# A hybrid attention and recurrence layer on one core: three heads of values in 512 columns, aligned pools, new costs for the placing clock

## The chip, the cores and the metric

The kernel runs on one core of a Trainium2 chip. The metric is device time in microseconds (us) from start to end of one launch. A core has TensorE (PE, matrix products into the banks of PSUM), VectorE (DVE), ScalarE (ACT), GpSimd (POOL) and SyncE (SP); PE's weight loads (PEld) run beside its products, and DMA queues move data between the chip's memory and SBUF.

## The reference

One layer over 512 latent tokens and 256 context tokens of width 2048, in float32:

```python
parts = split(hn @ w_in)                 # hn: modulated rmsnorm of latent or context tokens
q, k, v = heads(parts[0..2])             # 4 heads, 256 wide for q and k, 512 for v
o_gla, s_f, s_b = gla_bidir(q, k, v, la_f, la_b, s0_f, s0_b)
y_rnn = rglru_bidir(depthwise_conv(parts[6]), ...)      # 16 blocks of 128 channels
o = rmsnorm(o_gla) * silu(parts[3])
y = sigmoid(parts[8] + b) * (o @ w_o_gla) + sigmoid(parts[9] + b) * ((y_rnn * silu(parts[7])) @ w_o_rnn)
x = rmsnorm(x + gt_x * (y @ w_out)) * g_final
```

The modulation (`sh`, `sc`, `gt`) is a product of a conditioning vector with a 2048 by 6144 matrix. Context tokens pass the projection, the attention and the recurrence too, and their final states start the latent scans.

## The kernel before

Every large product is made of three: both operands are split into a high and a low part, and `mm3` issues high by high, low by high, high by low. Weights come as pieces of 128 x 1024 (512 KB): `run` loads a piece into `raw` (two buffers), ScalarE copies it rounded (`whi`), VectorE takes the difference (`wlo`), both in a `ring` of three, two pieces ahead of use. In the trace `L90` is any ScalarE activation, `L94` any VectorE tensor-tensor, `L127` any product through `mm`, so the tiles tell operations apart. A row `px<-whi,xhi ... 128x256` is a product into the bank `px` with 256 columns of `whi` streaming past tokens that are the loaded weights; `px<-xhi,whi` has tokens streaming.

The order on TensorE is the program's. It runs: the start (token norms, modulation, keys); a first phase with recurrent inputs (`g_feat`), values (`g_tok`, W_V: four token blocks of latents in two `px` banks, context in one `pc` bank, 256 columns, so eight groups for four heads), pieces of the gate matrix; the GLA phase from `to_gla` on; from `swap` on the two output projections; the final projection (`g_final`, four blocks of 512 columns). `VALUES_AT` says behind which of the eight recurrent groups the value groups come.

Beside it, side steps (`rnn_block`, `gate_row`, `gla_all`, generators) are put between two products where the products `yield`. `run_side` decides by a clock `T` of its own: each operation adds a cost in `_op`, and a step is taken when its inputs are ready by that clock. `need` and `flush_side` force the steps that are left: `to_gla` flushes at the end of the first phase, `swap` ahead of the first piece of `y`.

Side steps that matter here: a recurrent block makes two gates, each by three products `rx` and three `rc` into the single banks `sa` and `sb`, which a sigmoid (`g<-rx`) frees. `evac_v` copies values to staging tiles `vt` (two buffers) and stores them to `vS`. `gate_row` sums a weighted matrix (`pr<-gacc`, bank `sa`), copies it to `grow` (one buffer) and stores it to `rS`. `gla_out` makes a head's output (`po`), its norm (`ors`), scales it (`on`), transposes it (`pt`) and multiplies it into `sgg`.

Of the kernel before, what the change touches and what calls it, by code (L numbers as in the profile page):

```python
# [44 lines left out]

VALUES_AT = [(), (0,), (1,), (2,), (3,), (4,), (), (5, 6, 7)]

# [7 lines left out]
class Kern:  # L55
# [39 lines left out]

    def ts(self, out, in0, s1, s2=None, op0=ALU.mult, op1=None):
        self._op("dve", self._n(out) / 960.0 + 0.08, out, in0, s1)
        if op1 is None:
            return self.nc.vector.tensor_scalar(out=out, in0=in0, scalar1=s1, scalar2=None, op0=op0)
        return self.nc.vector.tensor_scalar(out=out, in0=in0, scalar1=s1, scalar2=s2, op0=op0, op1=op1)  # L100

    def stt(self, out, in0, s, in1, op0, op1):
        self._op("dve", self._n(out) / 960.0 + 0.08, out, in0, in1)
        return self.nc.vector.scalar_tensor_tensor(out=out, in0=in0, scalar=s, in1=in1, op0=op0, op1=op1)  # L104

    def scan(self, out, a, u, init):
        self._op("dve", self._n(out) / 480.0 + 0.08, out, a, u)
# [164 lines left out]
    def g_tok(self, w0, evac):  # L272
# [27 lines left out]
        return ps  # L300


    def build(self):
# [31 lines left out]
        self.cp = const.tile([P, 32], F32, name="cp")  # L335
        self.sm = open_pool("sm", bufs=2)

# [16 lines left out]
        def to_rnn():  # L354
            close_pool("raw0")
            close_pool("start")
            late = open_pool("late", bufs=1, side="right")
            self.mask = late.tile([P, 384], F32, name="mask")
            self.lax = late.tile([P, TA], F32R, name="lax")
            nc.gpsimd.memset(self.mask, 1.0)  # L360
            nc.gpsimd.memset(self.mask.rearrange("p (b t) -> p b t", t=P)[:, :, 0:1], 0.0)
            self.rp = open_pool("rnn", bufs=1)
            self.side.append(self.decay_consts())
            self.gacc = self.rp.tile([P, 1024], F32, tag="gacc", name="gacc")

# [3 lines left out]
        for j in range(8):  # L369
            main += self.g_feat(W_R + 4 * j, self.evac_r(j), True)  # L370
            main += self.g_feat(W_GR + 4 * j, self.evac_gr(j), False)
            for i in VALUES_AT[j]:
                main += self.g_tok(W_V + 4 * i, self.evac_v(i))
        gp = self.gate_pieces()
# [85 lines left out]
    def start(self, sp, raw0, raw, prime):  # L460
# [74 lines left out]
        sb_free = [0.0]  # L535
        pr0 = self.ps.tile([P, 4, 2], F32, tag="sb", name="pr")

# [4 lines left out]
        def squares(i, t):  # L542
            if i < 8:
                q = self.ring.tile([P, 1024], F32R, tag="whi", name="sq").bitcast(F32)
                h = self.ring.tile([P, 1024], F32R, tag="wlo", name="sh").bitcast(F32)[:, 0:512]
# [23 lines left out]
        def sums(i, h, r):  # L569

            for j in range(4):
                nc.tensor.matmul(pr0[:, j, :], lhsT=h[:, j * P:(j + 1) * P], rhs=ones[:, 0:2],
                                 start=i == 0 and j == 0, stop=i == 7, skip_group_check=True)
            t = pe("pr", 0.9, r)
            if i == 7:
                rstd(0, pr0, t)
# [7 lines left out]
        def rstd(s, pr, t):  # L584
            n = width[s] // P
            q = sp.tile([P, 4], F32, tag="rq", name="rq")[:, 0:n]
            self.rstd(q, pr[:, :, 0], D, sp.tile([P, 2, 4], F32, tag="rt", name="rt")[:, :, 0:n])
            t = sb_free[0] = at("dve", 0.4, t + 0.1)
            at("act", 0.2, t)
# [5 lines left out]
            t = at("dve", 0.22 * n, t)  # L595
            hot.append((lambda: max(t, sb_free[0]), lambda: spread(s, g, t)))

        def spread(s, g, r):

            w = width[s]  # L600
            pr = self.ps.tile([P, w], F32, tag="sb", name="pr")
            nc.tensor.matmul(pr, lhsT=ones, rhs=g[:, 0:w], start=True, stop=True)
            t = pe("pr", w / 600 + 0.05, r, sb_free[0])
            nc.scalar.activation(out=rms[s], in_=pr, func=AF.Copy)
            sb_free[0] = tok_ok[s] = at("act", w / 1200 + 0.18, t + 0.1)

# [305 lines left out]
    def evac_v(self, j):  # L912
        def f(c, x0, x1):
            h, o = j // 2, (j % 2) * 256
            for i, t in enumerate((c, x0, x1)):
                s = self.rp.tile([P, 2, 256], F32, tag="stg", name="vt", bufs=2)
# [570 lines left out]
    def g_final(self, j):  # L1487
# [30 lines left out]
        def evac(t, then=None):  # L1518
# [5 lines left out]
            if then:  # L1524
                then()
            self.act(self.junk, xr, AF.Square, accum_out=self.fss[:, t, j:j + 1])
            if j < 3:
                self.tt(xr, xr, self.gf[:, c0:c0 + 512], ALU.mult)

        held = []  # L1530
        for pi in range(8):
            def mm(hi, lo, pi=pi):
# [8 lines left out]
                if j == 0:  # L1541
                    loads(pi)
                if j == 0 and pi == 6:
                    nc.gpsimd.tensor_tensor(out=self.gt, in0=self.gt, in1=self.gb, op=ALU.add)
                if j == 3 and pi >= 5:
                    held.append((pi, hi, lo))
                    if pi == 7:
                        rest = None
                        for t in range(4):
# [5 lines left out]
                for t in range(4):  # L1555
                    mm_k(t, pi, hi, lo)

            def post():
                if j < 3:
                    for t in range(4):  # L1560
                        evac(t)
                if j == 2:

                    f = self.fss
                    self.fsum = self.sm.tile([P, 4], F32, tag="fsum", name="fsum")
                    self.tt(self.fsum, f[:, :, 0], f[:, :, 1], ALU.add)
                    self.stt(self.fsum, self.fsum, EPS * D, f[:, :, 2], ALU.add, ALU.add)
            ps.append(Piece(a["w"][W_OUT + 8 * j + pi], mm, post if pi == 7 else None))
# [33 lines left out]
def pack(i):  # L1602
# [14 lines left out]
    c = lambda a, b: w_in[:, a:b]  # L1617
    w = np.concatenate([
        c(1024, 2048).reshape(KT, P, 1024), g256(c(2048, 4096)), g256(c(6176, 8224)), g256(c(8224, 10272)),
        g256(c(0, 1024)), g256(c(4096, 6144)), g256(c(10272, 12320)), g256(c(12320, 14368)),  # L1620
# [54 lines left out]
```

## Time and profile before

| | |
|---|---|
| median of three runs | 2302.43 us (2301.64 to 2302.9) |
| profiled execution | 2307.69 us |
| its span, first to last instruction | 2306.0 us |
| mean granted TensorE clock | 0.997 |
| busy: PE, PEld, DVE, ACT, POOL | 99%, 84%, 50%, 44%, 5% |
| mean DMA rate over the span | 131 GB/s |

The span is what the views below show; the profiled execution is 5.26 us longer than the median. TensorE is nearly always busy, so its own waits, and the distances between the starts of its products, are what to read.

### The profile page before, as it was taken

What the parts mean: (1) busy time and instruction counts of PE and PEld (TensorE: products, weight loads), DVE (VectorE), ACT (ScalarE), POOL (GpSimd) and SP (SyncE); (2) the same over time, 40 slices, a digit from 0 to 9 for tenths busy, and PEclk for the clock granted to TensorE, in tenths of its full rate; (3) what the DMA queues carried; (4) which work ended last, traced back from release to release, by engine and by line L of the source; (5) the groups of instructions that cost most, each with busy time, mean ns of one, the idle gap of its engine ahead of it and who ended that gap; (6) DMA issues with size and microseconds to landing.
All of it is one profiled execution on the core that took longest, in us unless ns stands there. A gap on an engine that the chain in (4) does not pass through costs nothing. (4 is left out here: it accounts for less than half of the span.)

```text
span 2306.0 us, 29334 instructions
## 1 busy us (share of the span) xinstructions
PE 2275.4 (99%) x12064; PEld 1928.6 (84%) x12064; DVE 1163.2 (50%) x1494; ACT 1016.3 (44%) x1334; POOL 105.5 (5%) x201
## 2 busy tenths in 40 slices
PE   8999999999999999999999999999999999999998
PEld 5588889989898988998888888888888888888786
DVE  3563245655566555646637637647623432443335
ACT  4343255454454455456556555555533312222223
POOL 0010000000000000000000000000000000000000
PEclk9999999999999999999999999999999999999999
DMA  9943222333333332233233233323335533334423
GB/s 392 375 165 127 92 79 90 129 120 110 105 106 128 124 112 81 100 113 115 90 106 124 83 106 127 119 74 110 132 114 197 192 123 115 127 113 150 173 101 119
DMA packets 85814, 303.02 MB, mean 131 GB/s; under 512 B 10416, under 2 KB 11568, under 8 KB 84784
## 3 DMA queue, kind: packets, MB, share of 16 engines
q1 hardware_dynamic: 72656, 255.78, 32.0%
q0 software_dynamic: 13024, 45.37, 5.5%
q8 instruction: 94, 1.54, 0.3%
q14 instruction: 40, 0.33, 0.0%
HBM read 270.69 MB, written 30.42 MB: 131 GB/s over the span
## 5 line engine op out<-in xcount | busy, mean ns | idle before, releaser
L94 DVE TENSOR_TENSOR wlo<-raw,whi 128x1024 fp32r<-128x1024 f32 x304 | 371.9, 1224 | 568.1 <-ACT whi L90 566.8
L90 ACT ACTIVATE whi<-raw 128x1024 fp32r<-128x1024 f32 x304 | 321.0, 1057 | 529.8 <-PE px L127 327.3
L127 PE MATMUL px<-xhi,whi 128*128 128x512 f32 x1408 | 551.5, 392 | 0.0
L127 PE MATMUL px<-xhi,wlo 128*128 128x512 f32 x1408 | 549.1, 390 | 0.0
L127 PE MATMUL px<-xlo,whi 128*128 128x512 f32 x1408 | 548.1, 389 | 0.0
L127 PEld LDWEIGHTS px<-xhi,wlo 128*128 128x128 f32 x1408 | 264.2, 188 | 57.5 <-DVE wlo L94 0.2
L127 PEld LDWEIGHTS px<-xhi,whi 128*128 128x128 f32 x1408 | 264.4, 188 | 53.9 <-issue 2.6
L127 PEld LDWEIGHTS px<-xlo,whi 128*128 128x128 f32 x1408 | 264.5, 188 | 51.6
L127 PE MATMUL px<-whi,xhi 128*128 128x256 f32 x512 | 144.8, 283 | 0.0
L127 PE MATMUL px<-wlo,xhi 128*128 128x256 f32 x512 | 144.8, 283 | 0.0
L127 PE MATMUL px<-whi,xlo 128*128 128x256 f32 x512 | 144.7, 283 | 0.0
L90 ACT ACT_TABLE_LOAD x100 | 128.3, 1283 | 1.7
L127 PE MATMUL px<-whi,mhi 128*128 128x512 f32 x256 | 100.7, 393 | 2.3 <-ACT whi L90 2.3
L127 PE MATMUL px<-wlo,mhi 128*128 128x512 f32 x256 | 101.0, 394 | 0.8 <-DVE wlo L94 0.8
L127 PE MATMUL px<-whi,mlo 128*128 128x512 f32 x256 | 100.7, 393 | 0.0
L127 PE MATMUL px<-yhi,whi 128*128 128x512 f32 x256 | 99.6, 389 | 0.0
L127 PE MATMUL px<-ylo,whi 128*128 128x512 f32 x256 | 99.6, 389 | 0.0
L127 PE MATMUL px<-yhi,wlo 128*128 128x512 f32 x256 | 99.6, 389 | 0.0
L127 PE MATMUL px<-ohi,whi 128*128 128x512 f32 x256 | 99.6, 389 | 0.0
L127 PE MATMUL px<-olo,whi 128*128 128x512 f32 x256 | 99.6, 389 | 0.0
L127 PE MATMUL px<-ohi,wlo 128*128 128x512 f32 x256 | 99.6, 389 | 0.0
L127 PEld LDWEIGHTS px<-wlo,xhi 128*128 128x128 f32 x512 | 98.1, 192 | 0.2
(327 smaller groups left out, 3963.6 us busy)
## 6 DMA issues: line engine op xcount, KB each, us to landing
raw<-in_w SPq DMA_DIRECT2D x304, 512.0 KB, 3.6
araw<-in_wss SPq DMA_DIRECT2D x35, 512.0 KB, 8.9
raw<-in_wgt SPq DMA_DIRECT2D x32, 512.0 KB, 4.2
tok<-in_wss SPq DMA_DIRECT2D x29, 512.0 KB, 8.9
kraw<-in_w POOLq DMA_DIRECT2D x16, 512.0 KB, 3.9
gS<-mst POOLq DMA_DIRECT2D x32, 256.0 KB, 2.5
gst<-gS POOLq DMA_DIRECT2D x32, 256.0 KB, 3.0
vS<-vt POOLq DMA_DIRECT2D x24, 256.0 KB, 2.6
```

The costliest lines, as they stand in the source:

```text
L90: return self.nc.scalar.activation(out=out, in_=in_, func=func, **kw)
L94: return self.nc.vector.tensor_tensor(out=out, in0=in0, in1=in1, op=op)
L127: self.nc.tensor.matmul(out, lhsT=lhsT, rhs=rhs, start=start, stop=stop, skip_group_check=True)
```

## The change

It has five parts. Values: heads 0, 1 and 3 are made by a new `g_head`, whose four latent and two context token blocks each fill a bank with 512 columns and which yields between products; head 2 stays two narrow groups. The groups come behind other recurrent groups than before. The clock's costs: VectorE and ScalarE operations and products are counted longer. Pools: `sm` goes to the other side of SBUF, the recurrent pool's tiles are allocated ahead in an order of sizes and a filler tile is dropped, so that the context tokens and the recurrent and GLA tiles start at other addresses. Start: the squares of two token tiles are added before they are summed on TensorE. Final projection: gains and biases of the residual are loaded and added earlier, and squares and gain products of the first three blocks become a side step.

```diff
-VALUES_AT = [(), (0,), (1,), (2,), (3,), (4,), (), (5, 6, 7)]
+VALUES_AT = [(), (("w", 0),), (), (("w", 1),), (), (("n", 4),), (), (("w", 3), ("n", 5))]
...
-        self._op("act", self._n(in_) / 1200.0 + 0.2 + sw, out, in_)
+        ap = sum(not isinstance(kw.get(k, 0.0), (int, float)) for k in ("scale", "bias"))
+        self._op("act", self._n(in_) / 1200.0 + 0.2 + 0.07 * ap + sw, out, in_)
...
-        self._op("dve", self._n(out) / 960.0 + 0.08, out, in0, in1)
+        self._op("dve", self._n(out) / 960.0 + 0.16, out, in0, in1)
...
-        self._op("pe", (n / 2400.0 + 0.003 if n >= 256 else 0.213) / share, out, lhsT, rhs)
+        self._op("pe", (n / 2400.0 + 0.0135 if n >= 256 else 0.213) / share, out, lhsT, rhs)
...
+    def g_head(self, w0, evac):
...
+                if pi == 0:
+                    st["o"] = [self.px.tile([P, 512], F32, tag="px", name="px") for _ in range(4)] + \
+                              [self.pc.tile([P, 512], F32, tag="pc", name="pc") for _ in range(2)]
+                for t in (0, 1, 4, 2, 3, 5):
+                    xh, xl = (self.xhi, self.xlo) if t < 4 else (self.chi, self.clo)
+                    t0 = (t % 4) * P
+                    for kk in range(2):
+                        if t or kk:
+                            yield
+                        k = 2 * pi + kk
+                        self.mm3(st["o"][t], (xh[:, k, t0:t0 + P], xl[:, k, t0:t0 + P]),
+                                 (hi[:, kk * 512:(kk + 1) * 512], lo[:, kk * 512:(kk + 1) * 512]), k == 0, k == KT - 1)
+                    if pi == 7:
+                        evac(t, st["o"][t])
...
-        self.sm = open_pool("sm", bufs=2)
+        self.sm = open_pool("sm", bufs=2, side="right")
...
-            yp.tile([P, 240], F32, name="fill")
...
-                nc.vector.tensor_tensor(out=h, in0=q[:, 0:512], in1=q[:, 512:1024], op=ALU.add)
-                f = at("dve", 0.7, e)
-                hot.append((lambda: f, lambda: sums(i, h, f)))
+                if i % 2 == 0:
+                    half.append(self.ring.tile([P, 1024], F32R, tag="wlo", name="sh").bitcast(F32)[:, 0:512])
+                    nc.vector.tensor_tensor(out=half[0], in0=q[:, 0:512], in1=q[:, 512:1024], op=ALU.add)
+                    at("dve", 0.7, e)
+                else:
+                    h = half.pop()
+                    for u in (q[:, 0:512], q[:, 512:1024]):
+                        nc.vector.tensor_tensor(out=h, in0=h, in1=u, op=ALU.add)
+                        f = at("dve", 0.7, e)
+                    hot.append((lambda: f, lambda: sums(i, h, f)))
...
+    def evac_head(self, h):
+        def f(t, x):
+            s = self.rp.tile([P, 512], F32, tag="stg", name="vt", bufs=2)
+            self.act(s, x)
+
+            self.nc.gpsimd.dma_start(out=self.vS[h, :, (t + 2) % 6, :], in_=s)
+        return f
...
-            row = self.rp.tile([1, 512], F32, tag="grow", name="grow")
+            row = self.rp.tile([P, 512], F32, tag="grow", name="grow")[0:1]
...
+            if pi == 0:
+                nc.sync.dma_start(out=self.gt, in_=self.rS.partition_broadcast(P))
+            elif pi == 1:
+                nc.sync.dma_start(out=self.gb, in_=a["bgt"].partition_broadcast(P))
             elif pi == 4:
-                nc.sync.dma_start(out=self.gt, in_=self.rS.partition_broadcast(P))
-            elif pi == 5:
-                nc.sync.dma_start(out=self.gb, in_=a["bgt"].partition_broadcast(P))
-            elif pi == 6:
                 nc.sync.dma_start(out=self.gf, in_=a["gfin"].partition_broadcast(P))
...
-            self.act(self.junk, xr, AF.Square, accum_out=self.fss[:, t, j:j + 1])
-            if j < 3:
+            if j == 3:
+                self.act(self.junk, xr, AF.Square, accum_out=self.fss[:, t, j:j + 1])
+
+        def squares():
+
+            c0 = j * 512
+            for t in range(4):
+                xr = self.xres[:, t, c0:c0 + 512]
+                self.act(self.junk, xr, AF.Square, accum_out=self.fss[:, t, j:j + 1])
                 self.tt(xr, xr, self.gf[:, c0:c0 + 512], ALU.mult)
+                yield 0
...
-                if j == 0 and pi == 6:
+                if j == 0 and pi == 3:
                     nc.gpsimd.tensor_tensor(out=self.gt, in0=self.gt, in1=self.gb, op=ALU.add)
...
                 for t in range(4):
                     mm_k(t, pi, hi, lo)
+                    yield
...
+                    self.side.append(squares())
```

The end of the first phase on TensorE, before: the last recurrent group lies among 256-column products of the last value group.

```order
L127 MATMUL px<-whi,xhi 128x256
L127 MATMUL px<-wlo,xhi 128x256
L127 MATMUL px<-whi,xlo 128x256
L127 MATMUL rx<-xh,wh 128x512
L127 MATMUL rx<-xl,wh 128x512
L127 MATMUL rx<-xh,wl 128x512
L127 MATMUL rc<-xh,wh 128x256
L127 MATMUL rc<-xl,wh 128x256
L127 MATMUL rc<-xh,wl 128x256
L127 MATMUL px<-whi,xhi 128x256
L127 MATMUL px<-wlo,xhi 128x256
L127 MATMUL px<-whi,xlo 128x256
```

Now, on the same engine, the last context product is followed by two groups one behind the other, and then (below these rows) by the first GLA piece:

```order
L129 MATMUL pc<-whi,clo 128x256
L129 MATMUL rx<-xh,wh 128x512
L129 MATMUL rx<-xl,wh 128x512
L129 MATMUL rx<-xh,wl 128x512
L129 MATMUL rc<-xh,wh 128x256
L129 MATMUL rc<-xl,wh 128x256
L129 MATMUL rc<-xh,wl 128x256
L129 MATMUL rx<-xh,wh 128x512
L129 MATMUL rx<-xl,wh 128x512
L129 MATMUL rx<-xh,wl 128x512
L129 MATMUL rc<-xh,wh 128x256
L129 MATMUL rc<-xl,wh 128x256
```

ScalarE at this place now: the copies of values and a split stand ahead of the sigmoids of the two groups (`g_7997` of the first, `g_8008` of the second).

```order
L92 ACTIVATE vt<-pc 128x512
L92 ACTIVATE vt<-px 128x512 x2
L92 ACTIVATE whi<-raw 128x1024
L92 ACTIVATE g_7997<-rx,par 128x512
L92 ACTIVATE g_7997<-rc,par 128x256
L92 ACTIVATE g_8008<-rx,par 128x512
L92 ACTIVATE g_8008<-rc,par 128x256
L92 ACTIVATE sgr<-gr 128x512
```

The end of GLA on TensorE, before: behind the last `po` come 30 products, the last of them here, then eight transposes of the fourth head, and the other eight in two places further on.

```order
L127 MATMUL px<-xhi,whi 128x512
L127 MATMUL px<-xlo,whi 128x512
L127 MATMUL px<-xhi,wlo 128x512
L1432 MATMUL pt<-ident,on 128x128 x8
L127 MATMUL px<-xhi,whi 128x512
L127 MATMUL px<-xlo,whi 128x512
L127 MATMUL px<-xhi,wlo 128x512
```

Now all sixteen transposes follow the last `po` directly:

```order
L129 MATMUL po<-ht,Ah 128x512 x2
L129 MATMUL po<-ht,Al 128x512
L1490 MATMUL pt<-ident,on 128x128 x16
L129 MATMUL px<-xhi,whi 128x512
L129 MATMUL px<-xlo,whi 128x512
L129 MATMUL px<-xhi,wlo 128x512
```

The two sums of a gate row stand side by side and a recurrent group directly behind them, in both halves; before, products lay between them in the first half.

## Rows read from the trace of the kernel before

**Rows 1.** The list of cores, and the page's part 1 (busy us, share, instructions).
```profile
core 0: 2306.0 us, clock 0.997
PE 2275.4 (99%) x12064; PEld 1928.6 (84%) x12064; DVE 1163.2 (50%) x1494; ACT 1016.3 (44%) x1334; POOL 105.5 (5%) x201
```
**Rows 2.** TensorE's waits: who, for whom, us in total, times, longest.
```profile
PE pr L572 <- DVE sh L548: 7.1, 1, 7.1
...
PE pr L1061 <- ACT grow L90: 0.7, 1, 0.7
```
**Rows 3.** Timeline of TensorE, narrow value products, then final projection: start, us, operation.
```profile
963.24 0.28 PE L127 MATMUL px<-whi,xhi 128*128 128x256 f32 x1
...
969.00 0.28 PE L127 MATMUL pc<-whi,chi 128*128 128x256 f32 x1
...
971.83 0.28 PE L127 MATMUL px<-whi,xhi 128*128 128x256 f32 x1
...
2145.01 0.39 PE L127 MATMUL px<-whi,mhi 128*128 128x512 f32 x1
...
2168.80 0.39 PE L127 MATMUL px<-whi,mhi 128*128 128x512 f32 x1
```
**Rows 4.** Timeline of TensorE, second block of the final projection; in brackets the idle time.
```profile
2169.94 0.39 PE L127 MATMUL px<-whi,mlo 128*128 128x512 f32 x1
2172.60 0.50 PE L127 MATMUL px<-whi,mhi 128*128 128x512 f32 x1 [2.27 <-ACT whi L90]
2173.86 0.80 PE L127 MATMUL px<-wlo,mhi 128*128 128x512 f32 x1 [0.76 <-DVE wlo L94]
...
2179.93 0.40 PE L127 MATMUL px<-whi,mhi 128*128 128x512 f32 x1
```
**Rows 5.** Timeline of VectorE at the first evacuation of the final projection.
```profile
2160.85 0.69 DVE L94 TENSOR_TENSOR yt<-px,gv 128x512 f32<-128x512 f32 x1 [4.49 <-POOL gv L1544]
```
**Rows 6.** One line's instructions; busy time in a stretch, the last three: clock, DMA share, GB/s.
```profile
L572 PE MATMUL pr<-ones,sh x64: 343/353/374, 7.1 to 21.7; 128*128 128x2 f32 x64
...
10.00:20.00 10.00, 10.00 (x52) 9.39 (x52) 3.97 (x6) 5.29 (x5) 0.00 (x0) 1.00 1.03 419
```
**Rows 7.** Timeline of TensorE and ScalarE at 1010 us; waits ahead of tile vt.
```profile
1010.32 0.40 PE L127 MATMUL px<-xhi,whi 128*128 128x512 f32 x1
...
1014.07 0.60 ACT L90 ACTIVATE vt<-px 128x512 f32<-128x512 f32 x1 [2.46 <-DMA vS<-vt]
1014.56 2.27 ACT L90 ACTIVATE whi<-raw 128x1024 fp32r<-128x1024 f32 x2
...
  DMA vS<-vt: 21.5, 8
```
**Rows 8.** Timelines of TensorE and VectorE, output of the fourth head.
```profile
1656.87 0.40 PE L127 MATMUL px<-xhi,whi 128*128 128x512 f32 x1
...
1669.99 1.22 DVE L94 TENSOR_TENSOR ht<-st,ht 128x1024 fp32r<-128x1024 f32 x1
...
1690.94 0.39 PE L127 MATMUL px<-xhi,whi 128*128 128x512 f32 x1
...
1694.44 1.41 DVE L99 TENSOR_SCALAR on<-po,ors 128x512 f32<-128x512 f32 x2
...
1697.76 1.03 PE L1432 MATMUL pt<-ident,on 128*128 128x128 f32 x8
...
1698.39 0.69 DVE L94 TENSOR_TENSOR sgg<-pt,sgg 128x512 f32<-128x512 f32 x1 [1.07 <-PE pt L1432]
```
**Rows 9.** Timelines of TensorE and ScalarE at the gate rows of both halves.
```profile
620.97 0.59 ACT L90 ACTIVATE grow<-pr 1x512 f32<-1x512 f32 x1 [4.33 <-DMA rS<-grow]
...
621.61 0.50 PE L127 MATMUL rx<-xh,wh 128*128 128x512 f32 x1 [1.46 <-ACT grow L90]
...
622.65 0.28 PE L127 MATMUL rc<-xh,wl 128*128 128x256 f32 x1
...
887.57 0.59 ACT L90 ACTIVATE grow<-pr 1x512 f32<-1x512 f32 x1 [1.94 <-DMA rS<-grow]
```

More of the change, by code (lines that the diff above doesn't have):

```diff
@@ L102, in stt @@
     def stt(self, out, in0, s, in1, op0, op1):
-        self._op("dve", self._n(out) / 960.0 + 0.08, out, in0, in1)
+        self._op("dve", self._n(out) / 960.0 + 0.21, out, in0, in1)
         return self.nc.vector.scalar_tensor_tensor(out=out, in0=in0, scalar=s, in1=in1, op0=op0, op1=op1)
     def scan(self, out, a, u, init):
-        self._op("dve", self._n(out) / 480.0 + 0.08, out, a, u)
+        self._op("dve", self._n(out) / 480.0 + 0.16, out, a, u)
         return self.nc.vector.tensor_tensor_scan(
@@ L300, in g_tok, with mk, mm @@
         return ps
+    def g_head(self, w0, evac):
+        st = {}
+        ps = []
+        def mk(pi):
+            def mm(hi, lo):
+                if pi == 0:
[12 more added lines that the diff above has]
+                        evac(t, st["o"][t])
+            return mm
+        for pi in range(8):
+            ps.append(Piece(self.a["w"][w0 + pi], mk(pi)))
+        return ps
     def build(self):
@@ L362, in to_rnn @@
             self.rp = open_pool("rnn", bufs=1)
+            rp = self.rp
+            self.gacc = rp.tile([P, 1024], F32, tag="gacc", name="gacc")
+            for n, w, d, m in (("wh", 512, F32R, 1), ("wl", 512, F32R, 1), ("wr", 512, F32, 1), ("gr", TX, F32, 3),
+                               ("sgr", TX, F32, 2), ("stg", 512, F32, 2), ("grow", 512, F32, 1), ("xr", TA, F32, 3),
+                               ("xh", TA, F32R, 1), ("xc", TA, F32, 1), ("xl", TA, F32R, 1)):
+                rp.tile([P, w], d, tag=n, name=n + "0", bufs=m)
             self.side.append(self.decay_consts())
-            self.gacc = self.rp.tile([P, 1024], F32, tag="gacc", name="gacc")
         pcs[0].before = to_rnn
@@ L371, in build @@
             main += self.g_feat(W_GR + 4 * j, self.evac_gr(j), False)
-            for i in VALUES_AT[j]:
-                main += self.g_tok(W_V + 4 * i, self.evac_v(i))
+            for kind, i in VALUES_AT[j]:
+                if kind == "w":
+                    main += self.g_head(W_V + 8 * i, self.evac_head(i))
+                else:
+                    main += self.g_tok(W_V + 4 * i, self.evac_v(i))
         gp = self.gate_pieces()
@@ L535, in start @@
         sb_free = [0.0]
-        pr0 = self.ps.tile([P, 4, 2], F32, tag="sb", name="pr")
+        pr0 = self.px.tile([P, 4, 2], F32, tag="px", name="pr")
+        half = []
         def load_tok(i, d):
@@ L572, in sums @@
                 nc.tensor.matmul(pr0[:, j, :], lhsT=h[:, j * P:(j + 1) * P], rhs=ones[:, 0:2],
-                                 start=i == 0 and j == 0, stop=i == 7, skip_group_check=True)
-            t = pe("pr", 0.9, r)
+                                 start=i == 1 and j == 0, stop=i == 7, skip_group_check=True)
+            t = pe("pr", 1.87, r)
             if i == 7:
@@ L595, in rstd @@
             t = at("dve", 0.22 * n, t)
-            hot.append((lambda: max(t, sb_free[0]), lambda: spread(s, g, t)))
+            hot.append((lambda: max(t, sb_free[0] if s else 0.0), lambda: spread(s, g, t)))
         def spread(s, g, r):
             w = width[s]
-            pr = self.ps.tile([P, w], F32, tag="sb", name="pr")
+            pool, tag = (self.ps, "sb") if s else (self.px, "px")
+            pr = pool.tile([P, w], F32, tag=tag, name="pr")
             nc.tensor.matmul(pr, lhsT=ones, rhs=g[:, 0:w], start=True, stop=True)
-            t = pe("pr", w / 600 + 0.05, r, sb_free[0])
+            t = pe("pr", w / 600 + 0.05, r)
             nc.scalar.activation(out=rms[s], in_=pr, func=AF.Copy)
-            sb_free[0] = tok_ok[s] = at("act", w / 1200 + 0.18, t + 0.1)
+            tok_ok[s] = at("act", w / 1200 + 0.18, t + 0.4)
+            if s:
+                sb_free[0] = tok_ok[s]
         blocks = START_BLOCKS
@@ L1525, in evac @@
                 then()
-            self.act(self.junk, xr, AF.Square, accum_out=self.fss[:, t, j:j + 1])
-            if j < 3:
-                self.tt(xr, xr, self.gf[:, c0:c0 + 512], ALU.mult)
+            if j == 3:
[5 more added lines that the diff above has]
+                self.act(self.junk, xr, AF.Square, accum_out=self.fss[:, t, j:j + 1])
+                self.tt(xr, xr, self.gf[:, c0:c0 + 512], ALU.mult)
+                yield 0
+            if j == 2:
+                f = self.fss
+                self.fsum = self.sm.tile([P, 4], F32, tag="fsum", name="fsum")
+                self.tt(self.fsum, f[:, :, 0], f[:, :, 1], ALU.add)
+                self.stt(self.fsum, self.fsum, EPS * D, f[:, :, 2], ALU.add, ALU.add)
+                yield 0
         held = []
@@ L1617, in pack @@
     c = lambda a, b: w_in[:, a:b]
+    wv = [(g256 if h == 2 else g512)(c(2048 + 512 * h, 2560 + 512 * h)) for h in range(4)]
     w = np.concatenate([
-        c(1024, 2048).reshape(KT, P, 1024), g256(c(2048, 4096)), g256(c(6176, 8224)), g256(c(8224, 10272)),
+        c(1024, 2048).reshape(KT, P, 1024), *wv, g256(c(6176, 8224)), g256(c(8224, 10272)),
         g256(c(0, 1024)), g256(c(4096, 6144)), g256(c(10272, 12320)), g256(c(12320, 14368)),
```

16 lines of the change are left out of this document (7 added, 9 removed).

## The prediction, on record before the result

> **What bounds the kernel now.** The page's first part and the list of cores say that TensorE is busy 99% of the span at a granted clock of 0.997 [rows 1]. From some 85 us to the end the products follow one another, so a change is worth what it takes off that one stream: fewer or cheaper products, or idle time of that engine. VectorE and ScalarE, at about half the span, matter only where a product waits for them. The list of TensorE's waits, read second, is short: the first product of all waits 7.1 us, no other wait is over 2.5, and of the first phase only the gate sums and what follows them appear [rows 2]. Read third, the timeline of TensorE gives start-to-start distances; the "us" of one matmul overlaps the next and can't be used as a price.
>
> **Values.** Removed: six groups of 256 columns (three heads), 1152 products on the latent tokens and 576 on the context. Forty-eight latent ones take 963.24 to 969.00, 119.9 ns each; twenty-four context ones 969.00 to 971.83, 117.9 ns [rows 3]: 138.1 + 67.9 = 206.0 us. Added: 864 products of 512 columns. None with the weights as moving operand exists in this phase; the nearest are the output projection's (105 from 2145.01 to 2168.80, 226.6 ns [rows 3]): 195.8. Sum **-10** by these rows, -9.7 taken, since places between products cost a few weight switches. Bounds, with the distance two per cent to either side of that row: -14 and -6.
>
> Both widths carry about 13 ns over 256 and 512 columns at 2.4 GHz [rows 3], and it is that overhead which halving the count saves. The Trainium skill, "TensorE: Matmul & The Clock Gate", section "Wait — 56ns, not 53.3ns?", gives a fixed cost of about 2.5 ns for each matmul. By it 864 fewer would be worth 2.2 us instead of 9.7; no row here is that tight.
>
> **Final stage.** Before, the row of the residual's gain came in late; its POOL addition held VectorE 4.49 us, and VectorE began the four evacuations only at 2160.85 [rows 5]; ScalarE's next split stood behind them. TensorE's last product of that block started at 2169.94, the next at 2172.60, the one behind it at 2173.86, and until 2179.93 the clock was at its lower level [rows 4]. Between 2169.94 and 2179.93 sixteen products start; at 226.6 ns that is 3.63 us out of 9.99, so 6.36 are lost: 2.27 and 0.76 are the noted waits, the rest, about 3.2, is the clock. The change loads the gain at the first pieces, adds earlier, and leaves eight VectorE operations of 0.69 (5.5 us) ahead of the split, with squares and multiplication spread between later products. **-6.4** (0 if the early loads delay a split instead; the stream has two pieces of slack).
>
> **Start.** The sums are 64 passes in 7.1 to 21.7 [rows 6], 0.22 us each; 32 fewer would be 6.9. But the transfers run at 1.03 of the 16 engines in the same stretch [rows 6], and the pieces that follow land one by one, so the time freed mostly becomes a wait for them. **-1.5** (0 to -6.9).
>
> **The end of the first phase.** Now the two added parts. The new costs and order move the side steps, and a flush ahead of the GLA piece forces what is left. In the new order two recurrent-block groups (rx, rc) stand back to back behind the last context products, where 256-column products used to lie between groups. The second group needs the bank that the sigmoid of the first frees, and that sigmoid stands on ScalarE behind three copies of values and a split. How long these take is shown in the same place of before: TensorE is free at 1010.32, the third copy starts at 1014.07 (it waits 2.46 for the store of the first, whose staging buffer it takes), and the split at 1014.56 [rows 7]. This wait stands in all eight value groups, 21.5 us together [rows 7], hidden by products. With X for TensorE's first free moment: split at X+4.2, of one piece half the row's 2.27, and the sigmoid, as long as a copy of its shape (0.60) or a little longer, from 5.2 to 5.85; second group at X+5.9, where TensorE was ready at X+1.05: **+4.85** idle. A pause of 2.3 was followed by the lower clock [rows 4], so I add the price from there, **+3.2**. Behind the wait on ScalarE are the exponentials and the next split, needed some 24 us after X by my count and ready then: nothing is added.
>
> **The end of GLA.** Of the same kind. Before, 30 products lay between the last output product (po) of the last head and the first transposes (pt), and more between the transposes. Now the flush ahead of the first y piece puts all 16 transposes directly behind po. The chain to them, from E = 1690.94, the product after po: square, table, root, five small VectorE steps, and the scaling at 1694.44 (two take 1.41) [rows 8], so the first transpose at E+4.3. Then each tile passes transposes, VectorE's product 0.63 us after they start (1697.76, 1698.39) [rows 8], and the next scaling on the same engine, about 1.4 a tile: products resume at E+8.0. Less 1.75 of TensorE's own work: **+6.25**. One clock fall, **+3.2**. Ahead of it, 48 instead of 78 products stand between the last state products and po. The operand that po reads last was made by VectorE from 1669.99 on in 1.22, so ready 14.3 after TensorE left the state products at 1656.87 [rows 8]; 48 products are 10.9, the dozen of po that don't read it 2.7: late by **+0.7** (0 to 3).
>
> **Gate rows.** In before the two sums of a half were six products apart at the first half, adjacent at the second. The second row's copy waited for the store of the first, 4.33 us there and 1.94 at the second half [rows 9]; TensorE lost 1.46 in front of the recurrent group and 0.74 at the second half [rows 2, 9]. Now in both halves both sums and a recurrent group are adjacent. The second sum waits 0.74; the group waits for the gap of store (1.94 to 4.33, of which I take 2.5, the long one being one row), plus 0.59 of copy, less 1.0 of the sum itself: 1.5 to 3.9, taken 2.1. Two halves 5.7, less 2.2: **+3.5** (+2.3 to +7).
>
> **Addresses.** The pools move the context operand and the block weights to the alignment of the latent tokens. Context products at 117.9 ns were 2 ns shorter than the latent ones [rows 3]. If alignment sets that, some 1344 context products get 2.3 ns longer, 3.1; if alignment helps, 1 comes back. **+1.9** (-1 to 3.5). ScalarE's and VectorE's costs in the planner's clock are numbers of the plan alone; their effect is the order above.
>
> **Sum.** -9.7 -6.4 -1.5 +4.85 +3.2 +6.25 +3.2 +0.7 +3.5 +1.9 = +6.0. The profiled execution lasted 2307.69 (span 2306.0), 5.3 above the median of the three runs, and would become 2313.7; on the median, 2302.43 + 6.0 = 2308.4, 0.26% more. Changes below 0.2%, 4.6 us, can't be told from none: faster is below 2297.8, slower above 2307.0.
>
> **Rivals.**
> *The waits come without the clock falling.* The pause of 1.46 at the gate rows was followed by five products in 1.04 us, three wide and two narrow [rows 9], 0.12 more than at the full clock; one of 2.27 was followed by distances of 427 ns [rows 4]. Without the two falls: 2308.4 - 6.4 = 2302.0, no change. For it: the second new wait is broken by transposes. Against: both pauses are longer than the one that had the fall. Chance 0.2.
> *The forced steps find their results ready,* the other side. If the sigmoid is not held by the copies, or the norm of the last head is done under po, the idle and the clock of both places go (-18.2 with the 0.7): 2290.2, faster. It decides from the point where both places together cost less than 7.6 instead of 18.2. For it: before shows no forced step that waits. Against: the copies' wait occurs in all eight groups, and the norm needs the last po. Chance 0.15.
> *The gate rows and the phase's end cost more:* the store at 4.33 in both halves (+3.5), and a fall there or a late second split behind the exponentials (3 to 6): 2315 to 2318. Chance 0.12.
> *The wide products cost almost as much per column as the narrow,* as the page has it: +7.5, 2315.9. Beside the rows at 226.6 ns, chance 0.03.
>
> **How the numbers follow.** Chances: forecast 0.5, the rivals 0.2, 0.15, 0.12, 0.03. The forecast's own range, with start, addresses and the low half at their bounds, is 2302 to 2315; three tenths of it lie below 2307.0, hence 0.15 same and 0.35 slower from it. Same 0.15 + 0.18 = 0.33; slower 0.35 + 0.15 = 0.50; faster 0.17, from the second rival and the start at its full 6.9 beside the first. The range leaves out most of the second rival and the top of the third: 2293 to 2318.
>
> **What would show it.** Values right: distances of 226 to 228 ns in the wide groups, and TensorE's count down by 864 and 32. Final stage: no entry px <- whi or wlo in the list of waits, no lower clock near the second block of the output projection. The end of the first phase: an entry rx <- ACT of some 5 us there, with distances of 427 ns behind it. The end of GLA: pt <- DVE entries that add up to 6 us. Gate rows: rx <- grow twice, about 2 each. Addresses: context products at 120 instead of 118 ns. Start: the first recurrent products no more than 2 us earlier. The prediction is wrong if either flush shows no wait, or if the clock in the rows behind them stays at 2.4 GHz.

## The result: 0.8% slower, three times what was forecast

The changed kernel takes 2322.14 us (median of 4 runs, 2319.36 to 2322.49), the kernel before 2302.66 (4 runs); the ratio is 1.0081, 95% interval 1.0069 to 1.0094, so +15.9 to +21.6 us. The forecast was 2308.4, range 2293 to 2318. The direction and every place that it named were right; the sum was too small and the range ended below the result.

The changed kernel's cores and the page's busy time, in answer to [rows 1]:

```profile
core 0: 2317.7 us, clock 0.995
PE 2268.6 (98%) x11168; PEld 1886.0 (81%) x11168; DVE 1166.1 (50%) x1498; ACT 1019.4 (44%) x1336; POOL 101.1 (4%) x201
```

There are 896 products fewer, TensorE is busy 7 us less, and the span is 11.7 longer: the engine waits more. (The two profiled executions lie 5.0 above and 2.8 below the medians of four runs, hence 11.7 here and 19.5 between the medians.) Its list of waits (who, for whom, us in total, times, longest), in answer to [rows 2]:

```profile
PE pt L1490 <- DVE on L101: 6.7, 3, 4.1
PE rx L129 <- ACT grow L92: 5.5, 2, 3.6
PE rx L129 <- ACT g L92: 4.6, 1, 4.6
...
PE pr L1119 <- ACT grow L92: 1.3, 2, 0.7
PE px L129 <- ACT whi L92: 0.9, 1, 0.9
PE po L129 <- DVE ht L96: 0.8, 1, 0.8
PE pr L1119 <- DVE gacc L106: 0.7, 1, 0.7
```

The three forecast waits stand there by name: `pt <- on` and `rx <- g`, which the kernel before did not have, and `rx <- grow`, which it had at 1.5 us. `po <- ht` is 0.8 where 0.7 was computed. The end of the first phase, ScalarE and then TensorE, answers to [rows 7]:

```profile
1009.41 0.60 ACT L92 ACTIVATE vt<-px 128x512 f32<-128x512 f32 x1 [2.35 <-DMA vS<-vt]
1009.90 1.05 ACT L92 ACTIVATE whi<-raw 128x1024 fp32r<-128x1024 f32 x1
1010.85 0.68 ACT L92 ACTIVATE g<-rx,par 128x512 f32<-128x512 f32 x1
...
1006.70 0.28 PE L129 MATMUL rc<-xh,wl 128*128 128x256 f32 x1
1011.58 0.79 PE L129 MATMUL rx<-xh,wh 128*128 128x512 f32 x1 [4.60 <-ACT g L92]
1012.17 0.63 PE L129 MATMUL rx<-xl,wh 128*128 128x512 f32 x1
...
1014.78 0.39 PE L129 MATMUL px<-xhi,whi 128*128 128x512 f32 x1
```

The copy waits for its staging buffer, the split and the sigmoid follow, and the second recurrent group starts 4.88 after the last product of the first, at the lower clock (0.59 and 0.43 between starts) for 3 us. The end of GLA answers to [rows 8]:

```profile
1714.34 0.39 PE L129 MATMUL po<-ht,Al 128*128 128x512 f32 x1
1718.87 1.97 PE L1490 MATMUL pt<-ident,on 128*128 128x128 f32 x8 [4.15 <-DVE on L101]
1721.43 2.37 PE L1490 MATMUL pt<-ident,on 128*128 128x128 f32 x8 [0.59 <-DVE on L101]
1723.46 0.78 PE L129 MATMUL px<-xhi,whi 128*128 128x512 f32 x1
...
1727.87 0.44 PE L129 MATMUL px<-xlo,whi 128*128 128x512 f32 x1
```

Products resume 8.9 us after the slot behind `po` (1714.57), where E+8.0 was computed, and at the lower clock until 1727.87. The gate rows answer to [rows 9]:

```profile
614.91 0.39 PE L129 MATMUL px<-xhi,wlo 128*128 128x512 f32 x1
616.05 1.02 PE L1119 MATMUL pr<-gacc,ones 128*1 128x512 f32 x2 [0.75 <-DVE gacc L106]
617.75 1.02 PE L1119 MATMUL pr<-gacc,ones 128*1 128x512 f32 x2 [0.68 <-ACT grow L92]
622.37 0.80 PE L129 MATMUL rx<-xh,wh 128*128 128x512 f32 x1 [3.60 <-ACT grow L92]
```

From 614.91 to 622.37 the engine does one product and two sums of 1.02; the rest is the waits of the first sum, the second and the group. The values and the final stage run as planned in the changed kernel (what this is worth against before comes below); the first two rows bound 144 wide products, the last two the whole output projection, in answer to [rows 3, 4]:

```profile
539.98 0.40 PE L129 MATMUL px<-whi,xhi 128*128 128x512 f32 x1
...
572.64 0.39 PE L129 MATMUL rx<-xh,wh 128*128 128x512 f32 x1
...
2133.69 0.39 PE L129 MATMUL px<-whi,mhi 128*128 128x512 f32 x1
...
2307.55 0.39 PE L129 MATMUL px<-whi,mlo 128*128 128x512 f32 x1
```

144 products in 32.66 us are 226.8 ns each; the last stage is 173.86 long without a wait.

To compare executions, the stream is cut at four starts: the first product of the first phase, the first of GLA's queries, the first with `y`, the first of the output projection. Lengths in us, worked out from the timelines:

| | first phase | GLA | y to output | output |
|---|---|---|---|---|
| before, first trace | 800.97 | 757.29 | 348.16 | 180.23 |
| before, second trace (e10) | 799.23 | 757.28 | 348.16 | 174.51 |
| changed, first trace | 804.95 | 771.87 | 348.16 | 173.85 |
| changed, second trace (e9) | 808.49 | 770.15 | 348.16 | 173.85 |
| e2 heads alone | 799.89 | 767.68 | 348.16 | 177.89 |
| e3 costs alone | 802.97 | 772.03 | 348.16 | 175.89 |
| e6 two row buffers | 800.40 | 770.44 | 348.16 | 173.85 |
| e11 changed, old costs | 798.80 | 767.14 | 348.16 | 173.85 |

### The profile page after: what moved, and what is told of

The parts are those of the page before. It is cut to its first block, busy times and chain, and to the rows that moved or that the text cites. A ratio compares the mean times of both kernels' runs of the same rounds, so it can differ in the third digit from the quotient of the medians.

```text
span 2317.7 us, 27573 instructions
## 1 busy us (share of the span) xinstructions
PE 2268.6 (98%) x11168; PEld 1886.0 (81%) x11168; DVE 1166.1 (50%) x1498; ACT 1019.4 (44%) x1336; POOL 101.1 (4%) x201
## 3 DMA queue, kind: packets, MB, share of 16 engines
q8 instruction: 87, 1.43, 0.3%
## 4 chain that ended last, share of the span: by engine, by line
PE 68%; issue 25%; DVE 2%; ACT 2%; DMA 1%; POOL 1%; SPq 0%; DVEq 0%; POOLq 0%; ACTq 0%
PE px L129 53%; PE kx L882 4%; PE po L129 3%; PE kc L882 2%; PE pc L129 2%; PE pa L723 1%; PE pd L129 1%; PE pcs L129 1%; DMA araw<-in_wss 0%; DMA tok<-in_wss 0%; PE rx L129 0%; POOL vS L976 0%; POOL yS L1094 0%; DVE Z L110 0%; DVE wlo L96 0%
## 5 line engine op out<-in xcount | busy, mean ns | idle before, releaser
L129 PE MATMUL px<-whi,xhi 128*128 128x512 f32 (+1 forms) x320 | 111.2, 347 | 0.0
L129 PE MATMUL px<-wlo,xhi 128*128 128x512 f32 (+1 forms) x320 | 111.1, 347 | 0.0
L129 PE MATMUL px<-whi,xlo 128*128 128x512 f32 (+1 forms) x320 | 111.0, 347 | 0.0
L92 ACT ACTIVATE g<-rx,par 128x512 f32<-128x512 f32 x64 | 44.1, 689 | 111.4 <-PE rx L129 111.2
```

## The experiments

The theory is that of the prediction: steps forced behind one another make TensorE wait, and the clock falls behind the wait. Ratios are to the kernel before, run on the same chip.

**e1 to e4: one part of the diff at a time, on the kernel before.** e1 takes the edits of `g_final`, e2 those of `g_head`, `VALUES_AT` and `evac_head`, e3 those of the costs, e4 those of the pools:

```diff
+            if pi == 0:                                              # e1
+                nc.sync.dma_start(out=self.gt, in_=self.rS.partition_broadcast(P))
...
+                    main += self.g_head(W_V + 8 * i, self.evac_head(i))   # e2
...
+        self._op("dve", self._n(out) / 960.0 + 0.16, out, in0, in1)  # e3
...
+        self.sm = open_pool("sm", bufs=2, side="right")              # e4
```

> The kernel before with the part on the final projection alone. Theory (the wait at the second block and the lower clock behind it are lost time in every execution): 6.4 us shorter than before, 2296. Rival (the profiled execution of before, 5 us above its median, shows a fall of the clock that other executions do not have): 2 to 3.5 us shorter, 2299 to 2300.5. No change in the first phase or in GLA by either.

> The kernel before with the wide heads alone, at the old costs of the placing clock and with the old pools. Theory: -10 from the products; a wait of 4 to 5 us at the end of the first phase and one of 6 to 7 us at the end of GLA, both followed by the lower clock (3.2 each); the second pair of gate sums now has a recurrent group behind it, +2. Together +8 to +10: 2311. Rival (the planner's new costs make the waits, the heads only gain): 2293.

> The kernel before with the new costs of the placing clock alone. Theory: the order has all sixteen transposes behind the last output product and both sums of the first gate half side by side: +6.3 +3.2 +0.7 at the end of GLA, +2 to +4 at the gate, no wait at the end of the first phase; +12 to +14, 2315. Rival (costs closer to the measured durations place the steps better): no wait at either place, 2300 to 2303.

> The kernel before with the pools alone (addresses; the order of instructions is that of before). Theory: context products at 120 ns instead of 117.5 to 118, 1536 of them with values and 384 more of keys: +3 to +5, 2306. Rival (addresses cost nothing): 2302.5, within 0.1%. Second rival (they slow VectorE or ScalarE too): over +6.

e1: 2300.79, ratio 0.9990 (0.9981 to 0.9999): -2.3 us, the rival's value. e2: 2313.00, 1.0045 (1.0032 to 1.0057): +10.4, the theory's or a little over it. e3: 2318.34, 1.0065 (1.0051 to 1.0079): +15, a little over it. e4: 2303.82, 1.0006 (0.9997 to 1.0015): +1.4, below the theory's range, within the rival's 0.1% and within the noise. The part on the start has no run of its own. In the list of waits of e2 stand:

```profile
PE pt L1471 <- DVE on L100: 5.0, 2, 4.4
PE rx L128 <- ACT g L91: 4.7, 1, 4.7
...
PE rx L128 <- ACT grow L91: 1.5, 1, 1.5
```

and in that of e3, without any `rx <- g`:

```profile
PE pt L1433 <- DVE on L100: 6.7, 3, 4.1
...
PE rx L128 <- ACT grow L91: 2.1, 1, 2.1
```

The sixteen transposes are forced by either part; the wait at the end of the first phase needs the heads; the third wait of `pt` comes with the costs.

**e9, e10: the changed kernel and the one before, unaltered, for a second trace.**

> The changed kernel once more, for a second trace. Theory: the waits have the same length as in the first trace (rx <- g 4.6, pt <- on 6.7, rx <- grow 5.5), and what differs is how long the lower clock lasts behind them; the span is 2318 to 2321. Rival: another wait is longer by some us, at the start or at a transfer.

> The kernel before once more, for a second trace. Theory: the wait at the second block of the final projection is shorter than the 2.27 and 0.76 of the first trace, without the lower clock behind it, so that the stage from its first product is 175 to 177 us long instead of 180.2. Rival: the stage is as long as in the first trace, and the 5 us between that execution and the median lie at the start.

e9 took 2321.87 (one run); behind the start its waits of over 0.4 us are the first trace's to 0.1 us. The clock differs. A stretch with the second gate half, first trace (after start and end the busy time of five engines, then clock, DMA share, GB/s):

```profile
875.00:888.00 13.00, 10.44 (x44) 6.92 (x44) 2.61 (x3) 4.78 (x9) 1.02 (x2) 1.00 0.34 86
```

and e9:

```profile
880.00:892.00 12.00, 9.52 (x33) 6.05 (x33) 1.23 (x1) 3.90 (x7) 1.01 (x2) 0.86 0.36 104
```

A wait of 1.9 us was followed by the full clock, one of 1.8 by the lower; the first phase is 3.5 us longer in the second trace. e10 took 2301.42 (one run), and its output stage is 174.51, half a us under the expected 175 to 177: one short wait at full clock stands where [rows 4] show the long one.

```profile
2169.61 0.39 PE L127 MATMUL px<-whi,mhi 128*128 128x512 f32 x1
2170.36 0.50 PE L127 MATMUL px<-wlo,mhi 128*128 128x512 f32 x1 [0.36 <-DVE wlo L94]
```

Its gain rows were added on POOL from 2151.74 in 4.60, against 5.55 from 2155.27 in the first trace. POOL and a split on VectorE in the first trace, then in e10:

```profile
2155.27 5.55 POOL L1544 TENSOR_TENSOR gv<-gv 128x2048 f32<-128x2048 f32 x1 [59.49 <-DMA gv<-in_bgt]
2155.14 1.23 DVE L94 TENSOR_TENSOR wlo<-raw,whi 128x1024 fp32r<-128x1024 f32 x1 [4.21 <-ACT whi L90]
...
2151.74 4.60 POOL L1544 TENSOR_TENSOR gv<-gv 128x2048 f32<-128x2048 f32 x1 [56.52 <-DMA gv<-in_bgt]
2154.58 2.85 DVE L94 TENSOR_TENSOR wlo<-raw,whi 128x1024 fp32r<-128x1024 f32 x1 [4.22 <-ACT whi L90]
```

In e10 the DMA ahead of the addition landed earlier, the addition ends 4.5 us earlier, and ScalarE's split behind the evacuations starts 3.5 us earlier (2168.00 against 2171.50).

**e5, e16: the flushes two pieces later, both, and that of `y` alone.**

```diff
-        main[0].before = to_gla
+        main[2].before = to_gla                    # e5
...
-        n = len(main) - 8
-        for i in range(8):
+        n = len(main) - 6                          # e5, e16
+        for i in range(6):
             main.insert(n + 2 * i + 1, cy[i])
...
-                main += g
+                main += [g[0], cy[6], g[1], cy[7], g[2], g[3]]
```

> The changed kernel with both flushes two pieces (48 products, 10.9 us) later: the GLA pools are opened ahead of the third piece of the phase, and the first piece of y is loaded two pieces later. In its order no two recurrent groups stand side by side any more, the third head's first transposes and the second's have more products ahead of them, and 12 products stand between the last output product and the transposes. Theory (the two forced waits, with the clock behind them, and the places of the steps they displace are what the change loses): the entry rx <- g vanishes (-4.9 and 1.3 to 3.2 of clock), pt <- on falls from 6.7 to about 2 to 4, po <- ht vanishes: 12 to 16 us shorter than the changed kernel, 2306 to 2310. Rival (the loss is spread over the stream through addresses and ScalarE's load): 2318 or more.

> The changed kernel with the first piece of y two pieces later and nothing else; its order has 12 products between the last output product and the sixteen transposes, and 84 instead of 48 ahead of that output. Theory: po <- ht vanishes (-1), pt <- on at the last head falls by the 2.7 us that the twelve products take, to 3 to 4, and the lower clock there goes or is shorter: 4 to 7 us shorter than the changed kernel, 2315 to 2318. Rival (the first product of y is late instead): 2320 or more.

e5: 2312.97, 1.0050 (1.0037 to 1.0063), 7 us shorter than the changed kernel by the ratios and 9 by the medians, short of the 12 expected. `rx <- g` is gone, but opening GLA late makes its first product wait (`pz`, 1.3), and the transposes still alternate with VectorE behind their twelve products (5.7 in four waits). e16: 2320.46, 1.0082 (1.0068 to 1.0095), no difference that these runs can tell (3 us to either side), against an expected 4 to 7. In its trace GLA takes 767.6, which is 2.6 to 4.3 less than in the two traces of the changed kernel. More did not come: the first wait at the last head fell from 4.15 to 1.43, but those between the transposes grew from 0.59 to 2.18 (1.74 and 0.44). Twelve products ahead of the chain help little where the chain itself alternates between two engines.

**e6: two buffers for the gate's row.**

```diff
-            row = self.rp.tile([P, 512], F32, tag="grow", name="grow")[0:1]
+            row = self.rp.tile([P, 512], F32, tag="grow", name="grow", bufs=2)[0:1]
```

> The changed kernel with two buffers instead of one for the gate's row; the order of instructions is unchanged. Theory: the recurrent group behind the sums waits for the copies alone, not for the store: rx <- grow falls from 5.5 to about 1.5, and the lower clock behind it goes: 4 to 7 us shorter, 2315 to 2318. Rival (the sums' bank holds the group anyway): no change, 2322.

2314.27, 1.0057 (1.0044 to 1.0069): 5.5 us shorter than the changed kernel by the ratios and 8 by the medians, the theory's value. The order is the same; only the store is out of the way. Its timeline of TensorE at the first gate half:

```profile
619.62 1.02 PE L1119 MATMUL pr<-gacc,ones 128*1 128x512 f32 x2 [0.68 <-ACT grow L92]
621.31 0.50 PE L129 MATMUL rx<-xh,wh 128*128 128x512 f32 x1 [0.68 <-ACT grow L92]
```

**e11, e13, e14, e15: the costs of the placing clock.** The changed kernel with old costs (e11), with the new ones of VectorE and ScalarE only (e13), with that of a product only (e14), and e14 with two row buffers (e15). The product's is:

```diff
-        self._op("pe", (n / 2400.0 + 0.003 if n >= 256 else 0.213) / share, out, lhsT, rhs)
+        self._op("pe", (n / 2400.0 + 0.0135 if n >= 256 else 0.213) / share, out, lhsT, rhs)
```

> The changed kernel with the old costs of the placing clock: heads, pools, start and final stage as changed. Its order is that of the heads alone: the two recurrent groups and the sixteen transposes stand as in the changed kernel, the sums of the first gate half lie apart again, and the second and third heads' steps stand elsewhere. Theory (the heads alone force both waits, the costs add the first gate half, the wait at the third head and those of two splits): 2302.5 + 10.4 - 2.3 + 1.3 - 0.6 = 2311, 10 less than the changed kernel. Rival (the costs matter only where they force, and heads force already): 2318 to 2322.

> The changed kernel with the new costs of VectorE and ScalarE, but the old cost of a product. In its order eighteen and then twenty-four recurrent products stand together at the end of the first phase, and sixteen transposes behind the last output product with 24 products ahead of it. Theory (the clock places a step when TensorE's time has passed the side engines'; longer side costs alone make it lag, and the flushes force more): slower than the changed kernel, by one to three more waits of 2 to 5 us with their clock, 2326 to 2335. Rival (which costs are raised makes no difference): 2322.

> The changed kernel with the new cost of a product alone, VectorE's and ScalarE's as before. In its order no recurrent groups stand together, 30 products stand ahead of the last transposes; the sums of the first gate half still have a recurrent group behind them. Theory: no wait at either flush; values -9.6, final stage -2.3, start and addresses about 0, the first gate half +6: 2297, 0.25% faster than before. Rival (the heads' evacuations or the wide banks hold the stream elsewhere): 2303 or more.

> The same with two buffers for the gate's row. Theory: the group behind the sums waits for the copies alone, 0.7 twice; 4 to 6 us shorter than with one buffer, 2291 to 2293, 0.4 to 0.5% faster than before. Rival (the store is not what the group waits for): 2297.

e11: 2307.94, 1.0025 (1.0016 to 1.0034), 3 better than expected: of the change's loss some 13 us are the new costs. e13: 2353.25, 1.0226 (1.0212 to 1.0239): the theory's direction, at more than twice its price (+31 us over the changed kernel, expected were 4 to 13). Its longest wait, in the timeline of TensorE, is for a whole recurrent block that the flush forces:

```profile
1021.53 0.79 PE L129 MATMUL rx<-xh,wh 128*128 128x512 f32 x1 [12.29 <-ACT wh L92]
```

e14: 2306.86, 1.0022 (1.0013 to 1.0031); expected were 2297, and this is the rival's 2303 or more. No step waits at either flush now, and GLA takes 759.3; but a group in the middle of the first phase was placed before its bank was free. The timelines of e14, TensorE, then ScalarE:

```profile
609.17 0.28 PE L128 MATMUL pc<-chi,wlo 128*128 128x256 f32 x1
613.56 0.50 PE L128 MATMUL rx<-xh,wh 128*128 128x512 f32 x1 [4.11 <-ACT g L91]
...
609.97 0.60 ACT L91 ACTIVATE vt<-pc 128x512 f32<-128x512 f32 x1 [1.25 <-DMA vS<-vt]
610.46 1.05 ACT L91 ACTIVATE whi<-raw 128x1024 fp32r<-128x1024 f32 x1
611.53 1.28 ACT L91 ACT_TABLE_LOAD   x1
612.82 0.69 ACT L91 ACTIVATE g<-rx,par 128x512 f32<-128x512 f32 x1
```

The plan has no cost for the store that holds the copies. e15: 2306.29, 1.0020 (1.0011 to 1.0029), no shorter than e14. The group's wait fell from 1.6 to 0.7, as the theory has it, but the sums' waits (`pr <- grow`, 2.8 in two) stayed, and so did the 4.1 in the middle of the phase.

**e7, e8, e12: wide heads without forced steps.** The change without its costs, with two row buffers and the late `y` of e16; the flush ahead of GLA two pieces later (e7, and e8 with the pools of before) or one (e12).

```diff
+        main[2].before = to_gla                    # e7, e8
...
+        main[1].before = to_gla                    # e12
```

> The change without its new costs of the placing clock, with both flushes two pieces later and two row buffers. Its order has 30 products ahead of the last head's transposes, as before had, and no recurrent groups side by side. Theory: wide values -9.7, final stage -2.3, start -0.6, addresses +1.3, gate rows 0 to +1: 2292, 0.5% faster than before. Rival (wide values save less than the rows say, or hold the evacuations up): 2297 or more.

> The same as the kernel beside it (no new costs, late flushes, two row buffers), with the pools of before. Theory (aligned context operands cost 2 ns a product): 1 to 3 us shorter than that one, 2289 to 2291. Rival (addresses cost nothing, or the aligned tiles gain elsewhere): the same or longer.

> The change without its new costs, with two row buffers, the first piece of y two pieces later as in the kernel with late flushes, and the flush ahead of the GLA pools only one piece (24 products, 5.4 us) later instead of two. The order has no recurrent groups side by side and 30 products ahead of the last transposes. Theory (the wait pz <- issue of 2.3 us, with the lower clock behind it, came from opening the GLA pools late): it shrinks to under 0.5; 2 to 4 us shorter than with two pieces, 2294 to 2296, 0.3% faster than before. Rival (that wait is set by the pools' first transfer alone): 2298.

e7: 2298.16, 0.9981 (0.9973 to 0.9990). e8: 2299.54, 0.9990 (0.9981 to 0.9999), not shorter but 1.4 longer, with overlapping intervals. e12: 2297.27, 0.9978 (0.9969 to 0.9987), the fastest, 5 us below before; it is not clearly shorter than e7, and its `pz` wait went while a split's wait of 2.1 came. All three stay short of the 2292 or so that the terms gave: the first phase gains 10 us (790 against 800), but GLA takes 764.6 to 765.7 instead of 757.3, of which two recurrent groups that lie behind the late flush in all three are 2.1; so 8 of the 10 are gained. Most of the rest in e12 is four waits of TensorE, 4.1 together: 2.1, 0.9 and 0.5 for splits and 0.6 for a scaling.

The addresses' part shows in the mean length of one context product (the groups by line and shape; busy us, mean ns), 256 and 512 columns, in the changed kernel:

```profile
L129 PE MATMUL pc<-chi,wlo 128*128 128x256 f32 x256 | 72.6, 284 | 0.0
...
L129 PE MATMUL pc<-whi,chi 128*128 128x512 f32 x96 | 37.5, 390 | 0.0
```

and in e8:

```profile
L128 PE MATMUL pc<-chi,wlo 128*128 128x256 f32 x256 | 71.5, 279 | 0.0
...
L128 PE MATMUL pc<-whi,chi 128*128 128x512 f32 x96 | 38.0, 396 | 0.0
```

With the new addresses the narrow one is 5 ns longer and the wide one 6 ns shorter. These lengths overlap and are no price; between starts, in e7 beside e8, which differ by the pools alone, a narrow one is 2 ns longer (120 against 118) and a wide one 7 ns shorter (227.2 against 233.9).

## Why the prediction was wrong

| term | forecast | measured | by |
|---|---|---|---|
| values | -9.7 | -9.5 | 864 products at 227.4 ns (mean of all) against 206.0 us |
| final stage | -6.4 | -2.3 | e1 |
| start | -1.5 | -0.6 | first product of the first phase, first traces |
| end of the first phase | +8.05 | +6 | 4.60 idle, then 1.5 of lower clock |
| end of GLA | +10.15 | +14.6 and +12.9 | GLA's length, first trace and e9 |
| gate rows | +3.5 | +5 and +9 | waits of 7.5 less 2.2, then clock: under 1 in the first trace, 4 in e9 |
| addresses | +1.9 | +1.4 (-0.7 to 3.5) | e4 |
| sum | +6.0 | +15 and +17 | first trace and e9; whole change: +15.9 to +21.6 |

The mechanisms held. The rivals of ready results, of waits without the clock's fall and of dear wide products did not come; the third did at the first gate half, where the store took 4.04 instead of 2.5 and the clock fell. Three terms were mis-sized, all in one direction. A fourth hid a part of this: the fall behind the wait at the end of the first phase was priced at 3.2 and cost 1.5 (nine products from 1011.58 to 1014.78, 3.20 us instead of 1.72).

*Final stage, 4.1 us.* The step that failed is "6.36 are lost": a stall as long as that of [rows 4] belongs to the one execution that was profiled. That execution was 5.3 us above the median, which the prediction noted and then carried as an offset. The same stage took 174.5 in e10 and e4, 175.9 in e3 and 177.9 in e2, against 173.85 as changed. Of the 6.3 us between the first trace and e10 this stage holds 5.7: most of the offset was the stall.

*Gate rows, 2 to 6 us.* The store's gap was taken as 2.5, "the long one being one row", out of 1.94 and 4.33; in the changed kernel it was 4.04 in the first half. The fall of the clock behind it, and a sum that waits 0.75 for VectorE's accumulation, were not priced. The 4.33 and the 1.46 of [rows 9] are one execution's too: in e10 the gap there is 1.96, and TensorE waits 0.8 at both halves together instead of 2.2. e6, which takes the store alone away, gives 5.5 to 8 back.

*End of GLA, 3 to 4 us.* Forced transposes and the fall were sized well (first transpose at E+4.3: 1718.87 less 1714.57). Missed was the third head, which the prediction did not look at: the new costs put two scans of the next head between its scalings, and the transposes wait 2 us there too. ScalarE then waits for the store of the head before, and a split is late in both its parts (0.9 for ScalarE's, 0.5 for VectorE's). The changed kernel's timelines of VectorE and ScalarE there:

```profile
1583.29 1.80 DVE L110 TENSOR_TENSOR_SCAN Z<-mask,Z 128x384 f32<-128x384 f32 x2
1585.01 0.73 DVE L101 TENSOR_SCALAR on<-po,ors 128x512 f32<-128x512 f32 x1
...
1594.95 1.28 ACT L92 ACT_TABLE_LOAD   x1 [8.65 <-DMA oS<-sgg]
```

That the costs do this, and not the heads, is shown by e2 and e11 (GLA 767.7 and 767.1, no such waits; that is +10.4 and +9.9, the forecast +10.15) against e3 (772.0).

*What "numbers of the plan alone" hid.* The prediction read the costs only through two places of the order. e11, e13, e14 and the changed kernel are all four combinations: with both old 2307.94, with VectorE's and ScalarE's raised alone 2353.25 (+45), with the product's raised alone 2306.86 (-1, not told apart), with both raised 2322.14. VectorE's and ScalarE's at their longer values make the clock hold steps back until a flush forces them; the product's longer value lets them go earlier and takes 31 of the 45 back. Both raised together, the lag won. With the product's alone, a step went too early in the middle of the first phase.

The weighed rule, 2.5 ns a product by the Trainium skill ("TensorE: Matmul & The Clock Gate", section "Wait — 56ns, not 53.3ns?"), did not decide here: the wide products carry 13.5 ns over 512 columns at 2.4 GHz, and the first phase of e12 is 10 us shorter.

Left open: what decides in one execution whether the clock falls behind a pause of some 2 us, and what the part on the start is worth by itself.

## What to carry to other kernels

Where a plan's clock decides which step goes where, compare the two orders at every forced point and at every repetition of a loop, not at the two worst, and fit the costs of all engines together with the stores that hold buffers. If the profiled execution is longer than the median, look for the term in which that difference lies before it is counted as a gain. A wait that the stream has no cover for costs its length and, behind the three longest of the changed kernel (3.60, 4.15 and 4.60), the clock's fall. One more buffer for a stored row gave back over half of what the reshaped values save (e6), but nothing where the group also waited for something else (e15).

## What the runs showed of the hardware

The clock behind a pause is not a function of the pause's length alone: besides the second gate half (e9), the wait of 1.96 us at the third head was followed by products 227 ns apart in both traces of the changed kernel and by 427 ns in those of e5 and e16. POOL's 2048-column addition of gains and a split on VectorE met in all 18 traces, and the one that began second took longer. In the first trace the split began 0.13 earlier and kept its 1.23, and the addition took 5.55. In the 17 others the addition began first and took 4.60 to 4.62, and the split took 2.85 to 4.63 and ended 1.08 or 1.09 behind the addition each time, as if it had begun only then. And moving the operands to other addresses, by the pools alone, moved a context product in opposite directions by its width: 118 to 120 ns with 256 columns, 233.9 to 227.2 with 512 (e8, e7). Latents and context together, 129 wide products took 29.75 us (230.6 ns) with the old pools in e8, against 226.8 in the changed kernel; the first and last row in e8's timeline:

```profile
920.24 0.40 PE L128 MATMUL px<-whi,xhi 128*128 128x512 f32 x1
...
949.99 0.40 PE L128 MATMUL rx<-xh,wh 128*128 128x512 f32 x1
```
